# RMSNorm and matrix product on one core: TensorE's program for tiles 12 to 123 as a loop of sixteen tiles

## The chip, the cores and the metric

The kernel runs on one core of one Trainium2 chip. The metric is the device time of one execution in microseconds; the time of a kernel is the median of its runs.

## The reference

```
x: 16 x 1024 x 512 (f32)   gamma: 512   weight: 512 x 768   eps: 1e-5
rms    = sqrt(mean(x**2, axis=-1, keepdims=True) + eps)
x_norm = x / rms * gamma
out    = matmul(x_norm, weight)          # 16 x 1024 x 768, f32
```

## The kernel before

The 16,384 rows of x are 128 tiles of 128 rows. Two tiles are a pair `j`; the main loop runs over the pairs 1 to 63. Gamma is multiplied into the weights once, and the division by the rms is done on the product's rows when they leave PSUM. A tile goes through these steps:

- SyncE loads x in groups of 16 tiles (some in halves of 8) into two buffers `xt`.
- GpSimd casts x to bf16 (`cast`, into `xb`; `cast_quad`, into `xq`).
- ScalarE sums the squares of each row (`square`), two tiles at each pair, four pairs ahead, and takes the root of some tiles together (`root`); VectorE takes the reciprocal (`rstd`).
- x has to be turned so that features lie on the partitions. For 12 of every 16 tiles TensorE does it (`transpose_word`, four for each pair, strewn between the products by `feeder`) and VectorE copies the result from PSUM to `xT` (`evac`). For the last four tiles of a group of 16 (a quad, from tile 28 on) VectorE does it alone: sixteen 32x32-block transposes (`move`), three at each pair, into `xTq`.
- TensorE multiplies (`matmuls`): for each of four 128-feature slices one weight load (`hold`) and two products (`product`), 512 and 256 columns wide, into two PSUM banks that together hold a 128x768 result.
- `finish_tile` scales the result by `rstd` into `ot`: even tiles on ScalarE, odd tiles on VectorE. `store` sends eight tiles together to HBM through SyncE; the last tiles go in groups of 4, 4, 4, 2 and 2.

PSUM has three accumulators `ops` of two banks each, and two banks `tp` for transposes. `accumulator` deals the three out in turn, so a tile waits until the tile three before it has left PSUM.

Nothing is scheduled by a planner. The kernel is recorded as a list of operations with what each reads and writes (`Order.add`), in the order of the source. `Order.emit` works out which earlier operations each one has to wait for, gives each engine a semaphore that counts those of its operations that somebody waits for, and writes every engine's program straight out: 1,751 weight loads and matmuls on TensorE. Engines run their programs in order. SyncE's queue too is in order: a load that stands behind a store is issued after the store's wait has ended.

Of the kernel before, what the change touches and what calls it, by code (L numbers as in the profile page):

```python
# [11 lines left out]
F32 = mybir.dt.float32  # L12
BF16 = mybir.dt.bfloat16
# [3 lines left out]
P = 128  # L17
WIDE = 512


class Order:
# [1 line left out]

    def __init__(self, tc):  # L30
        self.tc, self.ops = tc, []

    def add(self, proc, engine, issue, reads=(), writes=()):
        self.ops.append((proc, engine, issue, list(reads), list(writes)))

    def transfer(self, engine, issue, reads=(), writes=()):
# [1 line left out]

    def emit(self):
        nc = self.tc.nc  # L40
        streams = {id(e): n for n, e in enumerate((nc.tensor, nc.vector, nc.scalar, nc.gpsimd, nc.sync))}
        writer, readers = {}, {}
        known = [dict() for _ in streams]
        clocks, needs, place, slot_of, slots = [], [], [], {}, []
        count = [0] * len(streams)
        for n, (proc, engine, _, reads, writes) in enumerate(self.ops):
            at = streams[id(engine)]
            if proc is None:
                me, turn = ("transfer", n), 1
            else:  # L50
                count[at] += 1
                me, turn = at, count[at]
            written = {writer[cell] for cell in reads + writes if cell in writer}
            read = {d for cell in writes for d in readers.get(cell, ())}
            need = []
            for d in sorted(written | read, reverse=True):
                who, when = place[d]
                if who == me and (engine is nc.tensor or d not in written):
                    continue
                if known[at].get(who, 0) < when:  # L60
                    need.append(d)
                    for k, v in clocks[d].items():
                        known[at][k] = max(known[at].get(k, 0), v)
            if proc is None:
                free = [k for k, d in enumerate(slots) if known[at].get(("transfer", d), 0)]
                if free:
                    slots[free[0]] = n
                else:
                    slots.append(n)
                slot_of[n] = ("slot", slots.index(n))  # L70
            clock = dict(known[at])
            clock[me] = turn
            place.append((me, turn))
            clocks.append(clock)
            needs.append(need)
            for cell in reads:
                readers.setdefault(cell, []).append(n)
            for cell in writes:
                writer[cell], readers[cell] = n, []
        awaited = {d for need in needs for d in need}  # L80
        seen = {who for clock in known for who in clock}
        last = [n for n, (me, _) in enumerate(place) if me not in seen and not isinstance(me, int)]
        sems, marks, done = {}, {}, {}
        for n in range(len(self.ops)):
            me = slot_of.get(n, place[n][0])
            if n in slot_of or n in awaited:
                if me not in sems:
                    sems[me] = self.tc.alloc_semaphore(f"done{len(sems)}")
                done[me] = done.get(me, 0) + (16 if n in slot_of else 1)
                marks[n] = (sems[me], done[me])  # L90
        for n, (proc, engine, issue, _, _) in enumerate(self.ops[:-1]):
            for d in needs[n]:
                engine.wait_ge(*marks[d])  # L93
            ins = issue()
            if n in marks:
                ins.then_inc(marks[n][0], 16 if n in slot_of else 1)
        return [marks[n] for n in last if n < len(self.ops) - 1], self.ops[-1][2]


@with_exitstack  # L100
def kernel(
# [8 lines left out]
    nc = tc.nc  # L110
    PE, DVE, ACT, POOL, SP = nc.tensor, nc.vector, nc.scalar, nc.gpsimd, nc.sync
    order = Order(tc)

    def run(engine, issue, reads=(), writes=()):
        order.add(1, engine, issue, reads, writes)

    x = x.flatten_outer_dims()
    out = out.flatten_outer_dims()
# [37 lines left out]
    jk = [sb(f"jk{n}", [P, D], BF16) for n in range(2)]  # L156
    xT = [sb(f"xT{n}", [P, 2, 2, P, 2], BF16) for n in range(4)]
    xq = [sb(f"xq{n}", [P, 4, D], BF16) for n in range(2)]
    xTq = [sb(f"xTq{n}", [P, 4, 2, P, 2], BF16) for n in range(2)]
    ot = [sb(f"ot{n}", [P, OG, O], F32) for n in range(3)]  # L160
    ssq = sb("ssq", [P, NT], F32)
    rms = sb("rms", [P, NT], F32)
    rstd = sb("rstd", [P, NT], F32)
# [70 lines left out]
    def evac(j, t=0, n=2):  # L234
        b = bank(j, t)
        src = tp[b].rearrange("p t h m -> p t (h m)").bitcast(BF16)
        dst = xT[j % 4].rearrange("p t h m c -> p t (h m c)")
        run(DVE, lambda: DVE.tensor_copy(out=dst[:, t:t + n, :], in_=src[:, t:t + n, :]),  # L238
            [("tp", b)], cells("xT", j % 4, t, n))
        for a in range(t, t + n):  # L240
            xT_of[2 * j + a] = (xT[j % 4][:, a], ("xT", j % 4, a))

    def transpose_tile(i):
        for h in range(2):
# [11 lines left out]
    def cast_quad(q):  # L256
        src, of = x_of(4 * q, 4)
        s = 4 * q // XG % 2
        run(POOL, lambda: POOL.tensor_copy(out=xq[s], in_=src), of, [("xq", s)])  # L259
        for t in range(4):  # L260
            xT_of[4 * q + t] = (xTq[s][:, t], ("xTq", s))
        words = xq[s].rearrange("p t d -> p (t d)").bitcast(F32).rearrange("p (a w) -> p a w", w=P)
        turned = xTq[s].rearrange("p t h m c -> p (t h m c)").bitcast(F32).rearrange("p (a m) -> p a m", m=P)
        for tokens in range(0, P, B):
            for features in range(0, P, B):
                quad_moves.append((turned[features:features + B, :, tokens:tokens + B],
                                   words[tokens:tokens + B, :, features:features + B], s))

    def move(dst, src, s):
        run(DVE, lambda: DVE.transpose(out=dst, in_=src), [("xq", s)], [("xTq", s)])  # L270

    def move_quad(n):
        for _ in range(min(n, len(quad_moves))):
# [5 lines left out]
        else:  # L279
            run(DVE, lambda: DVE.tensor_single_scalar(out=dst, in_=src, scalar=r, op=mybir.AluOpType.mult), reads, writes)  # L280

    turns = iter(range(NT + 1))

    def accumulator():
        return next(turns) % 3

    def store(i):
        first, n = o_first[i], o_size[i]
# [8 lines left out]
    def product(dst, lhsT, rhs, start, stop, reads, writes):  # L297

        run(PE, lambda: PE.add_instruction(mybir.InstMatmult(  # L299
            name=nc.get_next_instruction_name(), engine=mybir.EngineType.PE,  # L300
            ins=[PE.lower_ap(rhs), PE.lower_ap(lhsT)], outs=[PE.lower_ap(dst)],
            start_tensor_calc=start, stop_tensor_calc=stop, tile_size=(P, P), tile_position=(0, 0), ldweights=False)),
            reads, writes)

    def matmuls(i, a, ks, feed=None):
        block, cell = xT_of[i]
        for k in ks:
            lhsT = block[:, k // 2, :, k % 2]
            hold(lhsT, cell)
            for half, lo, hi in ((0, 0, WIDE), (1, WIDE, O)):  # L310
                product(ops[a][:, lo:hi], lhsT, w_bf[:, k, lo:hi], k == 0, k == K - 1,
                        [cell, ("w", k, half)], [("ops", a, half)])
            if feed:
                feed()

    def finish_tile(i, a, engine):
        s = i // OG % 3

        before = [("ot", s, i % OG - 1)] if i == o_first[i] + o_size[i] - 1 else []
        scale(engine, ot[s][:, i % OG, :], ops[a][:, :O], rstd[:, i:i + 1],  # L320
              [("ops", a, 0), ("ops", a, 1), ("rstd", i)] + before, [("ot", s, i % OG)])
        store(i)

    def feeder(pairs, gaps, alone=False):
        queue = [(j, t, h) for j in pairs for t in range(2) for h in range(2)]
# [17 lines left out]
    def load_weights(h):  # L343
# [10 lines left out]
    run(POOL, lambda: POOL.memset(ident_f, 0.0), [], ["ident"])  # L354
    run(POOL, lambda: POOL.affine_select(out=ident_f, in_=ident_f, compare_op=mybir.AluOpType.not_equal, fill=1.0, base=0,
                                         pattern=[[-1, P]], channel_multiplier=1), ["ident"], ["ident"])
    spare = accumulator()

    def warm_up(n):
        hold(warm[:, :P], "warm")  # L360
        for _ in range(n):
            product(ops[spare][:, :WIDE], warm[:, :P], warm, True, True, ["warm"], [("ops", spare, 0)])

    def weights(k, engine, lo=0, hi=O):
        halves = [half for half in range(2) if lo <= half * WIDE < hi]
# [19 lines left out]
    weights(0, DVE, 0, WIDE)  # L385
    weights(0, DVE, WIDE, O)
    weights(1, ACT)
    acc = [accumulator() for _ in range(2)]
    for i in range(2):
        matmuls(i, acc[i], [0, 1])  # L390
    weights(2, DVE)
    weights(3, ACT)
    norms(2, 2)
    cast(4, 2)
    matmuls(0, acc[0], [2, 3])
    finish_tile(0, acc[0], ACT)
    matmuls(1, acc[1], [2, 3], feeder([1], [2, 2], alone=True))
    finish_tile(1, acc[1], DVE)
    cast(6, 2)


# [2 lines left out]
    for j in range(1, NP):  # L404
# [17 lines left out]
        elif j == 3:  # L422
            feed = feeder([4, 5], both)
        elif j + 2 < NP and quad_of(j + 2) is None:
            feed = feeder([j + 2], two)
        else:
            feed = None
        for i, engine in ((2 * j, ACT), (2 * j + 1, DVE)):
            a = accumulator()
            matmuls(i, a, range(K), feed)  # L430
            finish_tile(i, a, engine)


    with tc.tile_critical():  # L434
# [45 lines left out]
```

## Time and profile before

| | |
|---|---|
| runs, device us | 208.79, 209.55, 209.25; median 209.25 |
| profiled execution, span | 207.5 us from the first to the last instruction, 1.7 us less than the median of the runs |
| busy: TensorE, VectorE, ScalarE, GpSimd | 193.3 us (93%), 149.3 (72%), 144.5 (70%), 59.8 (29%) |
| TensorE clock granted | 0.992 |
| DMA | 85.62 MB, mean 413 GB/s over the span |
| DMA queue of the loads and stores (q1) | its packets took 97.3% of 16 engines' span |
| instruction queues | q8: 7 packets, 0.11 MB; q14: 5 packets, 0.04 MB |

In the profile PE is a TensorE matmul, PEld its weight load, DVE VectorE, ACT ScalarE, POOL GpSimd and SP SyncE; L278 is line 278 of the kernel. The profile tells for each group of operations how long they were busy, how long the engine was idle ahead of them, and what ended that. It also tells for each DMA transfer when it was issued and when it had landed. A transfer of this kernel is marked as landed sixteen times, once for the share of each of the core's 16 DMA engines, and whoever waits for it waits for the last mark. Times in the trace are counted from the span's start.

### The profile page before, as it was taken

To read this page: it belongs to the slowest core of one execution; us is meant where nothing else is said; L and a number is where in the kernel's file an instruction comes from. 1 tells how busy PE (TensorE), PEld (TensorE's weight loads), DVE (VectorE), ACT (ScalarE), POOL (GpSimd) and SP (SyncE) were. 2 spreads that over 40 slices of the span, in tenths; PEclk is the share of its full clock that TensorE was granted. 3 is DMA by queue.
4 is the path that set the end of the run, shared out by engine and by line. 5 is a ranking of instruction groups with operands and counts; after the bars stand their busy time and mean duration, and the time that the engine had idled before them with its cause. 6 is when DMAs were issued, how large, how long until landed. Compare 5 with 4: busy or idle time off the path is not lost.

```text
span 207.5 us, 2761 instructions
## 1 busy us (share of the span) xinstructions
PE 193.3 (93%) x1212; PEld 72.6 (35%) x717; DVE 149.3 (72%) x255; ACT 144.5 (70%) x343; POOL 59.8 (29%) x34
## 2 busy tenths in 40 slices
PE   7779999999999999998999999999999999999940
PEld 1233434433443334342333333443334334433210
DVE  0446556999579966999379984999579984999530
ACT  4698897868777596763977877687867787683310
POOL 2156733009400291003900570006700175000000
PEclk9999999999999999999999999999999999999996
DMA  6999999999999999999999999999999999998993
GB/s 225 403 441 436 388 405 456 455 388 422 436 445 442 395 425 448 429 411 431 434 407 436 437 428 434 418 428 437 417 426 426 433 442 425 426 436 381 407 404 139
DMA packets 5632, 85.62 MB, mean 413 GB/s; under 512 B 626, under 2 KB 628, under 8 KB 1780
## 3 DMA queue, kind: packets, MB, share of 16 engines
q1 hardware_dynamic: 5616, 85.46, 97.3%
q8 instruction: 7, 0.11, 0.2%
q14 instruction: 5, 0.04, 0.0%
q10 hardware_dynamic: 4, 0.00, 0.0%
HBM read 35.13 MB, written 50.33 MB: 412 GB/s over the span
## 4 chain that ended last, share of the span: by engine, by line
PE 71%; DMA 16%; DVE 5%; issue 2%; SPq 1%; ACT 1%; POOL 1%; ACTq 0%
PE ps L299 62%; DMA xt<-in_x_dram 16%; PE ps L229 8%; DVE ot L280 2%; DVE xTq L270 2%; DVE xT L238 1%; SPq L344 1%; POOL xb L187 1%; ACT jk L195 0%; SPq L176 0%; ACT ot L278 0%; SPq L292 0%; DVE rstd L202 0%; SPq L475 0%; ACTq L93 0%
## 5 line engine op out<-in xcount | busy, mean ns | idle before, releaser
L299 PE MATMUL ps<-w_bf,xT 128*128 128x256 bf16 (+1 forms) x783 | 145.0, 325 | 3.4 <-ACT ot L278 1.3
L278 ACT ACTIVATE ot<-ps,rstd 128x768 f32<-128x768 f32 x64 | 57.4, 898 | 42.4 <-PE ps L299 40.5
L195 ACT ACTIVATE jk<-xt 128x512 bf16<-128x512 f32 x128 | 78.8, 619 | 8.3 <-DMA xt<-in_x_dram 8.2
L187 POOL CAST xb<-xt 128x2048 bf16<-128x2048 f32 (+3 forms) x21 | 46.3, 2218 | 113.2 <-DMA xt<-in_x_dram 111.4
L280 DVE TENSOR_SCALAR ot<-ps,rstd 128x768 f32<-128x768 f32 x64 | 64.8, 1013 | 9.9 <-PE ps L299 9.2
L295 PEld LDWEIGHTS <-xT 128*128 128x128 bf16 x400 | 39.3, 98 | 61.2 <-issue 53.2
L229 PE MATMUL ps<-ident_f,xb 128*128 128x128 f32 x200 | 54.4, 277 | 0.9 <-POOL xb L187 0.9
L238 DVE COPY xT<-ps 128x1024 bf16<-128x1024 bf16 (+1 forms) x53 | 34.5, 653 | 24.5 <-PE ps L229 22.8
L270 DVE STREAM_TRANSPOSE xTq<-xq 32x256 f32<-32x256 f32 x112 | 48.7, 435 | 3.4
L229 PEld LDWEIGHTS ps<-ident_f,xb 128*128 128x128 f32 x200 | 28.3, 143 | 46.5 <-issue 42.9
L299 PE MATMUL ps<-w_bf,xTq 128*128 128x256 bf16 (+1 forms) x217 | 41.8, 324 | 0.4
L195 ACT ACTIVATION_READ_ACCUMULATOR jk<-xt 128x1 f32 x128 | 24.3, 190 | 0.0
L295 PEld LDWEIGHTS <-xTq 128*128 128x128 bf16 x112 | 11.0, 98 | 14.5 <-issue 14.5
L259 POOL CAST xq<-xt 128x2048 bf16<-128x2048 f32 x7 | 13.3, 1893 | 0.0
L202 DVE RECIPROCAL rstd<-rms 128x8 f32<-128x8 f32 (+3 forms) x20 | 3.8, 192 | 7.9 <-ACT rms L200 7.7
L200 ACT ACTIVATE rms<-ssq,eps_sb 128x8 f32<-128x8 f32 (+3 forms) x20 | 6.0, 300 | 0.6
L299 PE MATMUL ps<-warm 128*128 128x512 bf16 x10 | 4.4, 582 | 1.4 <-DVE eps_sb L353 1.4
L278 ACT ACTIVATE w_bf<-w_f,g_sb 128x768 bf16<-128x768 f32 x2 | 1.9, 936 | 1.7 <-DMA w_f<-in_weight_dram 1.7
L376 DVE COPY g_sb<-ps 128x4 f32<-128x4 f32 x1 | 0.2, 163 | 3.2 <-PE ps L370 3.2
L340 ACT ACT_TABLE_LOAD x1 | 1.3, 1283 | 1.5 <-SPq L434 1.5
L280 DVE TENSOR_SCALAR w_bf<-w_f,g_sb 128x512 bf16<-128x512 f32 (+2 forms) x3 | 1.4, 481 | 1.1 <-DMA w_f<-in_weight_dram 1.1
L370 PEld LDWEIGHTS ps<-ident_f,g_row 2*128 2x128 f32 x2 | 0.3, 200 | 2.6 <-issue 2.6
(10 smaller groups left out, 2.0 us busy)
## 6 DMA issues: line engine op xcount, KB each, us to landing
out_dram<-ot SPq DMA_DIRECT2D x13, 3072.0 KB, 16.6
xt<-in_x_dram SPq DMA_DIRECT2D x9, 2048.0 KB, 21.1
xt<-in_x_dram SPq DMA_DIRECT2D x3, 4096.0 KB, 22.2
out_dram<-ot SPq DMA_DIRECT2D x4, 1536.0 KB, 11.3
out_dram<-ot SPq DMA_DIRECT2D x3, 768.0 KB, 7.0
w_f<-in_weight_dram SPq DMA_DIRECT2D x2, 768.0 KB, 5.8
xt<-in_x_dram SPq DMA_DIRECT2D x2, 512.0 KB, 5.2
xt<-in_x_dram SPq DMA_DIRECT2D x1, 1024.0 KB, 9.0
```

The source lines that it names most:

```text
L187: run(POOL, lambda: POOL.tensor_copy(out=xb[s][:, i % 8:i % 8 + n, :], in_=src), of, cells("xb", s, i % 8, n))
L195: run(ACT, lambda: ACT.activation(out=jk[j], in_=src[:, 0, :], func=AF.Square, accum_out=ssq[:, i:i + 1]), of, [("jk", j), ("ssq", i)])
L200: run(ACT, lambda: ACT.activation(out=rms[:, s], in_=ssq[:, s], func=AF.Sqrt, scale=1.0 / D, bias=eps_sb), [("ssq", t) for t in range(i, i ...
L202: run(DVE, lambda: DVE.reciprocal(out=rstd[:, s], in_=rms[:, s]), [("rms", i)], [("rstd", t) for t in range(i, i + n)])
L229: run(PE, lambda: PE.transpose(out=tp[b][:, t, h, :], in_=words[:, lo:lo + P], identity=ident_f), cells("xb", s, j % 4 * 2 + t) + ["ident" ...
L238: run(DVE, lambda: DVE.tensor_copy(out=dst[:, t:t + n, :], in_=src[:, t:t + n, :]), [("tp", b)], cells("xT", j % 4, t, n))
L259: run(POOL, lambda: POOL.tensor_copy(out=xq[s], in_=src), of, [("xq", s)])
L270: run(DVE, lambda: DVE.transpose(out=dst, in_=src), [("xq", s)], [("xTq", s)])
L278: run(ACT, lambda: ACT.mul(out=dst, in_=src, mul=r), reads, writes)
L280: run(DVE, lambda: DVE.tensor_single_scalar(out=dst, in_=src, scalar=r, op=mybir.AluOpType.mult), reads, writes)
L295: run(PE, lambda: PE.ldweights(lhsT), [cell])
L299: run(PE, lambda: PE.add_instruction(mybir.InstMatmult(name=nc.get_next_instruction_name(), engine=mybir.EngineType.PE, ins=[PE.lower_ap(r ...
```

## The change

`Order` now notes which TensorE operations belong to which turn of sixteen tiles (tiles 12 to 27 are the first, 108 to 123 the seventh) and to which half of a turn. `emit` writes TensorE's operations of the first turn once, inside a loop that runs seven times and whose head is placed at slot 0 of an instruction fetch block. TensorE's program shrinks from 1,751 weight loads and matmuls to 191 ahead of the loop, 216 in it and 48 behind it; the loop adds a counter's addition and a branch. All other engines' programs remain written out.

A loop can only wait for the same semaphore values in each turn. So:

- Operations of other engines that TensorE waits for inside the loop no longer count on their engine's common semaphore, but on one of their own for each engine and half of a turn. A product behind the last wait of a half takes the half's count off again (`taken`).
- Somebody else who waited for such an operation now waits for the next operation of that engine that is not of this kind (`shared`). For the stores this is the VectorE operation that comes after the scaling of the last tile of a group, nearly always one of the `move`s.
- Where VectorE scales the last tile of a store's group, it waited for ScalarE's scaling of the tile before. It now waits for a new small ScalarE operation behind that (`told`, one element on each partition), 20 in all.
- Each tile position of the turn has a fixed accumulator, by a list of sixteen. In it a tile takes up the accumulator of the tile three before, but for four places: the positions 6 and 8 take that of the tile two before, the positions 7 and 9 that of the tile four before. The positions 4, 6 and 8 are tiles that ScalarE scales.
- `xTq` has one buffer in place of two, and tiles 12 to 15, which TensorE transposes, use it too.

```diff
+        turns = sorted(self.body)
+        size = len(self.body[turns[0]])
 ...
+        waits = [sorted({place[d][0] for t in turns for d in needs[self.body[t][q][0]]}) for q in range(size)]
 ...
+        def shared(d):
+            if d not in events:
+                return d
+            return next(e for e in order[place[d][0]] if e > d and e not in events)
 ...
+        taken = {}
+        for (who, half), sem in own.items():
+            final = max(q for q, w in values if w == who and self.body[turns[0]][q][1] == half)
+            q = next(q for q in range(final + 1, size) if q not in flags and q not in taken and self.ops[self.body[turns[0]][q][0]][0] == "product")
+            taken[q] = (sem, -counts[who, half])
+
+        def give(n):
+            _, engine, issue, _, _ = self.ops[n]
             for d in needs[n]:
-                engine.wait_ge(*marks[d])
+                engine.wait_ge(*marks[shared(d)])
             ins = issue()
             if n in marks:
                 ins.then_inc(marks[n][0], 16 if n in slot_of else 1)
+            elif n in events:
+                ins.then_inc(own[place[n][0], events[n][1]], 1)
 ...
+        with nc.Fori(0, len(turns), engines=[mybir.EngineType.PE], head_slot={mybir.EngineType.PE: 0}):
+            for q, (n, half) in enumerate(self.body[turns[0]]):
+                for who in waits[q]:
+                    nc.tensor.wait_ge(own[who, half], values[q, who])
+                ins = self.ops[n][2]()
+                if n in marks:
+                    ins.then_inc(marks[n][0], 1)
+                elif q in taken:
+                    ins.then_inc(*taken[q])
+        for n in late:
+            give(n)
 ...
-    turns = iter(range(NT + 1))
-
-    def accumulator():
-        return next(turns) % 3
+    def accumulator(i):
+        return (2, 0, 1, 2, 0, 1, 0, 2, 0, 1, 2, 0, 1, 2, 0, 1)[(i - 12) % 16] if i >= 12 else (i + 2) % 3
 ...
-        before = [("ot", s, i % OG - 1)] if i == o_first[i] + o_size[i] - 1 else []
+        ends = i == o_first[i] + o_size[i] - 1 and i > o_first[i]
+        before = [("told", i - 1)] if ends else []
         scale(engine, ot[s][:, i % OG, :], ops[a][:, :O], rstd[:, i:i + 1],
               [("ops", a, 0), ("ops", a, 1), ("rstd", i)] + before, [("ot", s, i % OG)])
         store(i)
+        if engine is ACT and i + 1 == o_first[i] + o_size[i] - 1:
+            run(ACT, lambda: ACT.mul(out=told, in_=eps_sb, mul=1.0), ["eps"], ["told", ("told", i)])
 ...
+        order.turn, order.half = ((j - 6) // 8, (j - 6) % 8 // 4) if 6 <= j < NP - 2 else (None, 0)
```

## The prediction

> **What bounds the kernel now.** I read the page first, then who waited for whom, the stretch of one turn, and last the landing marks of the transfers. The page says that two things are nearly full at once:
>
> ```profile
> span 207.5 us, 2761 instructions
> PE 193.3 (93%) x1212; PEld 72.6 (35%) x717; DVE 149.3 (72%) x255; ACT 144.5 (70%) x343; POOL 59.8 (29%) x34
> q1 hardware_dynamic: 5616, 85.46, 97.3%
> q8 instruction: 7, 0.11, 0.2%
> q14 instruction: 5, 0.04, 0.0%
> ```
>
> TensorE is busy for 93%, the load and store queue for 97.3% of sixteen engines. The two instruction queues look like nothing: twelve packets. The waits say where TensorE loses time:
>
> ```profile
> ACT ot L278 <- PE ps L299: 40.5, 50, 1.9
> ACT jk L195 <- DMA xt<-in_x_dram: 8.2, 6, 3.6
> PE ps L299 <- ACT ot L278: 1.3, 1, 1.3
> ```
>
> That is next to nothing: one stop of 1.3 us, when ScalarE had stood 3.6 us for a late load of x. So nothing is to be won on TensorE itself. But what ends last? TensorE stops at 199.3, and the end of the trace reads:
>
> ```profile
> 199.38 1.02 DVE L280 TENSOR_SCALAR ot<-ps,rstd 128x768 f32<-128x768 f32 x1 [1.58 <-PE ps L299]
> 200.69 0.33 SPq L292 DMA_DIRECT2D out_dram<-ot  x1
> ```
>
> The last store, 768 KB, has its first landing mark at 203.9 and its last at 206.6. I took the sixteen marks of each transfer from the trace, first mark and spread from first to last, in us:
>
> ```
> transfer                  first mark   spread
> x, tiles 16 to 23              21.42     0.79
> x, tiles 24 to 31              26.65     2.51
> x, tiles 32 to 47              43.98     3.04
> x, tiles 64 to 79              92.48     4.26
> store, tiles 112 to 115       190.83     4.79
> store, tiles 126, 127         203.91     2.72
> ```
>
> The spread is 0.8 us until the first q8 packet, which starts at 27.1 us, and never less than 1.9 after it. The q8 packets are 16 KB each, start at 27.1, 50.1, 76.5, 103.5, 127.1, 151.0 and 175.9 us, and take 0.89 to 0.98 us. Following the packets of an engine back to back (the next one starts when the last ends), I find the sixteen engines' order: each q8 packet lies on another engine, and its engine falls behind by 1.3 to 1.4 us at once (at 151.0 us from 0.37 to 1.67), and by some 0.4 to 0.7 more at later loads of x. The engine that is last from 27 us on took the first q8 packet (it goes from 0.50 to 2.46) and no later one; three loads of x carry it on to 4.8. From there to the end it has no pause: the end of the kernel is this engine's backlog. The other engines do pause, about 2 us between 190 and 204. Next behind it come an engine with three of the q14 packets and one that drifts back with no fetch at all; in the last store they are 2.12 and 2.01 behind the first mark, the fourth 1.44. So TensorE has 2.7 us of room at the end: the last store could be issued that much later and the slowest engine would still be busy with earlier ones.
>
> **What it adds.** Seven additions and branches on TensorE's sequencer, and one branch to the loop's head. The nearest row is TensorE's own branch at 0.82 us, 0.17 us: 8 x 0.17 = 1.4 us in all if it lay open. [...] Branch cost: 0; without that cover 1.4 us, which the 2.7 us of room takes.
>
> The accumulators. A distance of four costs nothing. A distance of two, at 14 places, needs ScalarE to be through with a tile before TensorE has done the next. One such place is tile 96, and TensorE comes to tile 98 with the third product of the second row, at 155.92 + 0.32 = 156.24:
>
> ```profile
> 154.93 0.90 ACT L278 ACTIVATE ot<-ps,rstd 128x768 f32<-128x768 f32 x1 [0.92 <-PE ps L299]
> 155.92 0.81 PE L299 MATMUL ps<-w_bf,xT 128*128 128x512 bf16 x4
> ```
>
> ScalarE ends at 155.83: 0.41 us early. All other evacuations of these positions were released by TensorE too, with 0.92 us of idle ahead. Cost 0; if ScalarE were late by y, y - 0.41 at that place.
>
> The 20 `told` operations. Nearest rows: 0.19 us (the accumulator's reading) and 0.30 us (the root, 128x8). I take 0.25, 5 us on ScalarE, which was idle 40.5 us for TensorE and 0.58 to 0.92 ahead of the evacuations concerned. Only the last one is near the path: ScalarE ends tile 126 at 198.97, with `told` 199.2, and VectorE starts the last tile at 199.38. Cost 0, at worst 0.1.
>
> The stores wait for one more VectorE operation, a `move`, 0.435 us in its row, 16 times, and each load of x stands behind such a store in SyncE's queue, so it is issued 0.45 later. Stores land 16.6 us after issue, loads 21 us: they queue behind earlier transfers, and the slowest engine never runs dry. Cost 0; if the queue were dry, 0.45 once, since the two last stores wait as before. The single `xTq`: its first `move` stands behind the scaling of the quad's last tile on VectorE already. Cost 0.
>
> **What it removes.** [...] What that is worth depends on the engine that is last. If the fetch at 27 us goes, or lands where it does less, the next engine decides: 2.72 - 2.12 = 0.6 us. If all lag went, the last store would end 0.5 behind its first mark, as small stores do without lag (0.45 at the first load): 2.72 - 0.5 = 2.2 us. The q14 packets, which the change leaves, keep me near the lower end: 0.8 us. It must come out of the span 207.5, giving 206.7; with the 1.7 us that lie between span and median, 208.45.
>
> [...]
>
> **The rivals.** [...]
>
> (2) Slower: the fetch that stays falls on the engine that also serves the q14 packets. The six later ones were spread over six engines, so the choice moves. Price: 2.12 plus 1.3 to 2.0 is 3.4 to 4.1 us behind, against 2.72: 0.7 to 1.4 us, 209.95 to 210.65. It decides from a lag of 2.72 on.
>
> [...]
>
> (4) That the loop does not do what it says (TensorE's program still long) I rule out: 455 weight loads and matmuls are left.
>
> **How the numbers follow.** About 0.3% (0.63 us) is what a measurement of this kernel can tell from no change. Forecast, the last engine's lag falls: 0.40, value 208.45, own range 207.0 (all lag gone) to 208.65 (the next engine as it is). Rival 1: 0.33, 208.9 to 209.6. Rival 2: 0.15. Rival 3: 0.12. Faster 0.40, same 0.33, slower 0.15 + 0.12 = 0.27. The range is 207.0 to 210.6: it holds the forecast, rival 1 and nearly all of rival 2, and leaves out most of rival 3 and a gain beyond 2.2 us, some 0.15.
>
> **What would show it.** Right: q8 with two or three packets in place of seven, fewer engines more than 1 us behind, a spread in the last store of 2.1 us or less; the x load of tiles 64 to 79 landing before 96.7, and with it TensorE's stop of 1.3 us shorter (which alone doesn't move the end). Rival 1: the spread still 3.0 at tiles 32 to 47, 4.3 at tiles 64 to 79, 2.7 at the end. Rival 2: over 3.4 at the end. Rival 3: a gap of TensorE every 23.4 us and seven or more q8 packets. The prediction is wrong in its ground if the time moves by over 0.6 us while the last store's spread does not, or if TensorE waits for ScalarE once each turn.

## The result, and the profile after

The change makes the kernel slower by about 0.75 us: median 209.84 us (209.16 to 211.21) against 209.15 us (208.35 to 210.05) of the kernel before in the same measurement, a ratio of 1.0037 [1.0022, 1.0052]. The prediction said 208.45, faster; the time lies within its range, the sign is wrong. The profiled execution of the change took 210.62 us, longer than its median; a second profiled one (e1, the same kernel) took 209.44. Both are used below, and neither for a difference of the medians.

The page of the changed kernel, its busy times and DMA queues:

```profile
span 208.8 us, 2821 instructions
PE 194.5 (93%) x1236; PEld 72.7 (35%) x717; DVE 149.4 (72%) x255; ACT 146.2 (70%) x363; POOL 59.8 (29%) x34
q1 hardware_dynamic: 5616, 85.46, 97.4%
q8 instruction: 3, 0.05, 0.1%
q14 instruction: 5, 0.04, 0.0%
```

q8, whose 16 KB packets are fetches of instructions, has three packets in place of seven. ScalarE has 20 instructions more, the `told` operations. The waits of the same kernel (who waited, for whom; then us in all, times, longest):

```profile
ACT ot L348 <- PE ps L367: 41.2, 52, 1.8
ACT jk L262 <- DMA xt<-in_x_dram: 6.9, 5, 2.6
PE ps L367 <- DVE xTq L309: 1.2, 1, 1.2
PE ps L367 <- ACT ot L348: 0.4, 1, 0.4
```

TensorE's one stop for an accumulator that ScalarE had still to empty has fallen from 1.3 to 0.4 us (at 99 us in both kernels), and a new stop has come, once, for `xTq`. No wait belongs to `told` or to a branch back. Two turns of the loop, cut at the scalings of tiles 59 and 75 and of tiles 107 and 123 (length in us; the busy time of TensorE, its weight loads, VectorE, ScalarE and GpSimd; the granted TensorE clock, the busy share of the DMA engines and GB/s), first in the changed kernel and then the same tiles in the kernel before:

```profile
100.56:123.98 23.42, 23.42 (x153) 8.88 (x88) 19.07 (x33) 18.50 (x46) 9.02 (x4) 1.00 1.01 429
170.82:194.24 23.42, 23.42 (x153) 8.88 (x88) 19.07 (x33) 14.99 (x38) 3.73 (x2) 1.00 1.00 426
```

```profile
100.50:123.92 23.42, 23.26 (x150) 8.88 (x88) 19.07 (x33) 18.33 (x44) 10.00 (x5) 1.00 1.01 433
170.76:194.18 23.42, 23.26 (x150) 8.88 (x88) 19.08 (x33) 14.62 (x34) 3.27 (x2) 1.00 0.98 419
```

A turn takes 23.42 us with the loop and without (three matmul records of each turn are missing from the trace of before); in all 19 executions of the table below tile 127 is scaled 98.88 us after tile 59. TensorE's sequencer, which runs ahead of it, has these rows for the loop's branches (shortest, median and longest in ns, then the first and the last start):

```profile
L152 PEldq COMPARE_BRANCH  x8: 76/208/4585, 24.9 to 191.4; - x8
```

The six branches back take 0.21 to 0.24 us each on the sequencer and cost TensorE nothing; the shortest is the way out. The longest is the entry: the sequencer stands at it from 24.88 to 29.46 us. The end of the changed kernel:

```profile
198.94 0.19 ACT L394 ACTIVATE told<-eps_sb 128x1 f32<-128x1 f32 x1
199.44 1.02 DVE L350 TENSOR_SCALAR ot<-ps,rstd 128x768 f32<-128x768 f32 x1 [1.58 <-PE ps L367]
200.75 0.33 SPq L360 DMA_DIRECT2D out_dram<-ot  x1
```

The last store is issued at 200.75, before at 200.69. What has moved is its landing: the first mark at 203.97 (before 203.91), the last at 207.89 (before 206.63). The spread of the last store is 3.91 us in place of 2.72; 3.17 in the second profile.

### The profile page after: what moved, and what is told of

Read it like the earlier page. It is cut to its first block, busy times and chain, and to the rows that moved or that the text cites. A ratio compares the mean times of both kernels' runs of the same rounds, so it can differ in the third digit from the quotient of the medians.

```text
span 208.8 us, 2821 instructions
## 1 busy us (share of the span) xinstructions
PE 194.5 (93%) x1236; PEld 72.7 (35%) x717; DVE 149.4 (72%) x255; ACT 146.2 (70%) x363; POOL 59.8 (29%) x34
## 4 chain that ended last, share of the span: by engine, by line
PE 71%; DMA 15%; DVE 6%; issue 2%; SPq 1%; ACT 1%; POOL 1%; ACTq 0%
PE ps L367 62%; DMA xt<-in_x_dram 15%; PE ps L296 8%; DVE ot L350 2%; DVE xTq L340 2%; DVE xT L309 1%; POOL xb L254 1%; ACT jk L262 0%; SPq L416 0%; SPq L243 0%; ACT ot L348 0%; DVE xTq L309 0%; SPq L360 0%; DVE rstd L269 0%; SPq L544 0%
## 5 line engine op out<-in xcount | busy, mean ns | idle before, releaser
L367 PE MATMUL ps<-w_bf,xT 128*128 128x512 bf16 (+1 forms) x768 | 141.8, 326 | 1.4 <-DVE w_bf L350 0.9
L363 PEld LDWEIGHTS <-xT 128*128 128x128 bf16 x384 | 37.7, 98 | 58.2 <-issue 56.9
L367 PE MATMUL ps<-w_bf,xTq 128*128 128x512 bf16 (+1 forms) x256 | 49.0, 326 | 1.2 <-DVE xTq L309 1.2
L309 DVE COPY xT<-ps 128x1024 bf16<-128x1024 bf16 (+1 forms) x51 | 33.1, 652 | 23.1 <-PE ps L296 21.5
L363 PEld LDWEIGHTS <-xTq 128*128 128x128 bf16 x128 | 12.5, 98 | 17.8 <-issue 16.1
L394 ACT ACTIVATE told<-eps_sb 128x1 f32<-128x1 f32 x20 | 3.8, 192 | 0.0
L309 DVE COPY xTq<-ps 128x1024 bf16<-128x1024 bf16 x2 | 1.4, 692 | 2.4 <-PE ps L296 2.4
```

The source lines that it names most:

```text
L363: run(PE, lambda: PE.ldweights(lhsT), [cell])
L367: run(PE, lambda: PE.add_instruction(mybir.InstMatmult(name=nc.get_next_instruction_name(), engine=mybir.EngineType.PE, ins=[PE.lower_ap(r ...
```

## The experiments

Four theories stood at first. A: TensorE and with it the stores come later at tile 12, DMA engines run dry near 50 to 70 us, and the stream stays late. B: only the slowest of the sixteen DMA engines counts. C: the new accumulators, `told` and waits cost at many places. D: the loop itself costs. Ratios are to the kernel before on the same chip, 95% intervals behind them.

**e1, the change once more.** No edit.

> The changed kernel once more, beside the next three on the same chip. Theory A (TensorE stops 1.2 us at the loop's entry, because its sequencer waits for the block that holds the loop, and each store waits for one VectorE operation more; the DMA engines run out of work for 1.8 us between 50 and 70 us and never get that back): ratio to the kernel before 1.003 to 1.005, TensorE stops 1.0 to 1.5 us ahead of tile 12 again. Theory B (only the lag of the slowest DMA engine decides, by where the fetches fall): the ratio moves between chips, 1.000 to 1.006. Theory C (the new waits and accumulators cost a little everywhere): 1.0037.

1.0032 [1.0013, 1.0051]: the loss is there again. **e2**, the loop's head at slot 14 in place of slot 0:

```diff
-        with nc.Fori(..., head_slot={mybir.EngineType.PE: 0}):
+        with nc.Fori(..., head_slot={mybir.EngineType.PE: 14}):
```

> [...] Theory A: no stop of TensorE ahead of tile 12, two q8 packets in place of three, the first landing mark of the x load of tiles 48 to 63 near 68.8 us instead of 70.1; ratio to before 0.997 to 1.000. Theory B: the stop goes, the time stays, 1.002 to 1.005, unless the slowest engine's lag moves with it. Theory C: 1.0037.

1.0040 [1.0025, 1.0055], three q8 packets as in the change: the place of the head is not the cause.

**e3, the change with its loop written out**: all waits, accumulators and buffers of the change, but seven turns of code.

```diff
-        with nc.Fori(0, len(turns), ...):
-            for q, (n, half) in enumerate(self.body[turns[0]]):
+        for k, t in enumerate(turns):
+            for q, (n, half) in enumerate(self.body[t]):
-                    nc.tensor.wait_ge(own[who, half], values[q, who])
+                    nc.tensor.wait_ge(own[who, half], values[q, who] + k * counts[who, half])
 ...
```

> All of the change (semaphores of their own, accumulators in an order of sixteen, one xTq, told, the stores' later wait) without the loop: TensorE's seven turns are written out, with counts that go on rising. Theory A: no stop at tile 12, seven q8 packets, the stream of transfers 0.4 to 0.6 us late at the x load of tiles 48 to 63 from the stores' wait alone, the lag as before: ratio 1.001 to 1.003. Theory B: 1.000. Theory C: 1.0037.

1.0015 [1.0003, 1.0027]. More than half of the loss goes with the loop. The new stop at tile 12 has two parts, which the timelines show; the changed kernel first:

```profile
28.04 0.69 DVE L309 COPY xTq<-ps 128x1024 bf16<-128x1024 bf16 x1 [1.42 <-PE ps L296]
29.52 0.10 PEld L363 LDWEIGHTS <-xTq 128*128 128x128 bf16 x1 [1.69 <-DVE xTq L309]
```

Then e3, written out:

```profile
28.53 0.69 DVE L307 COPY xTq<-ps 128x1024 bf16<-128x1024 bf16 x1 [1.42 <-PE ps L294]
29.27 0.10 PEld L361 LDWEIGHTS <-xTq 128*128 128x128 bf16 x1 [0.95 <-DVE xTq L307]
```

Tile 12 waits for the copy of tiles 14 and 15, since the four tiles now share the one cell `xTq`. Written out, TensorE goes on 0.05 us after that copy has ended; in the loop 0.79 us after it (29.52 less 28.73), though the view names the copy for both. The sequencer's row above gives the rest of the wait: its branch into the loop ends at 29.46, 0.06 ahead of the weight load. By the scalings of tiles 11 and 13, which lie 3.04 us apart before, the stop is 1.37 us in the changed kernel, 1.01 in e1, 1.38 in e2 and 0.63 in e3: the shared cell is 0.63, the entry into the loop 0.4 to 0.75 (in e7 and e6 below it is 0.3 and 0; in e6 the branch ends ahead of the copy). Nothing of it repeats in later turns.

**e4, the kernel before with a stop put in**: a weight load and six products of zeros ahead of tile 12. **e5, the loop from tile 28**, six turns, tiles 12 to 15 back in `xT`. The edits of e4 and of e5 (of e5 the main line):

```diff
+            if i == 12:
+                hold(warm[:, :P], "warm")
+                for _ in range(6):
+                    product(ops[a][:, :WIDE], warm[:, :P], warm, True, True, ["warm"], [("ops", a, 0)])
```

```diff
 ...
-        order.turn, order.half = ((j - 6) // 8, (j - 6) % 8 // 4) if 6 <= j < NP - 2 else (None, 0)
+        order.turn, order.half = ((j - 14) // 8, (j - 6) % 8 // 4) if 14 <= j < NP - 2 else (None, 0)
```

> The kernel before, with one weight load and six products of 128x512 more (zeros, 1.3 us) on TensorE ahead of tile 12; nothing else. Theory A: the stores of tiles 8 to 23 leave 1.3 us later, the DMA engines run dry and the end moves by 1.0 to 1.3 us: ratio 1.005 to 1.006. Theory B, and the prediction's 2.7 us of room at the end: 1.000. Theory C says nothing on it.

> The loop begins one turn later: tiles 12 to 27 are written out, the loop covers tiles 28 to 123 in six turns, and tiles 12 to 15 go through xT again. Theory A, as the first four runs leave it (up to the store of tiles 16 to 23 the DMA engines wait for the stores, so a late TensorE moves all that follows; after it they never run dry. Late by 0.73 us for tile 12 waiting on the second pair in xTq, 0.4 to 0.75 for the loop's entry, 0.38 for the store waiting on a move): that store is issued near 48.7 us as in the kernel before, the stop at the entry comes at tile 28, where it is hidden; ratio 0.998 to 1.001. Theory D (the loop itself costs, by its fetches and by what its turns add): 1.002 to 1.004.

e4: 1.0017 [1.0004, 1.0030]; the load of x for tiles 48 to 63 begins to land at 69.24 in place of 68.21, so a shift of 1.0 us goes with 0.17%, 0.36 us (0.1 to 0.6 by the interval). e5: 1.0029 [1.0012, 1.0047], though that load lands at 68.28 and no stop is left. Theory A has a part of the loss at most. **e6** split the stores of the second and third group of eight in halves to have them leave sooner, **e8** did the same in the kernel before, **e7** let the stores wait for a small VectorE operation straight behind the scaling:

```diff
-    o_first, o_size = stretches(OG, {0: [1, 1, 2, 4], ...
+    o_first, o_size = stretches(OG, {0: [1, 1, 2, 4], 1: [4, 4], 2: [4, 4], ...
```

```diff
+    said = sb("said", [P, 1], F32)
 ...
+        if ends:
+            run(DVE, lambda: DVE.memset(said, 0.0), [], ["said"])
         store(i)
```

> The changed kernel with the stores of tiles 8 to 15 and 16 to 23 in halves of four tiles, nothing else: the DMA engines get the first half some 6 us earlier. The stops of TensorE stay. Theory A: the x load of tiles 48 to 63 has its first landing mark near 68.3 us instead of 69.5 to 70; ratio 0.998 to 1.001. Theory D: 1.003.

> The kernel before with the same split stores as in the run named split. In it the DMA engines ran dry for 0.14 us at that place, and not at all where TensorE stopped 1.3 us near 98 us. Theory A: little to gain, ratio 0.998 to 1.000. Theory D: 1.000. Should it gain as much as the split does in the changed kernel, the split acts otherwise than by closing the gap.

> The changed kernel with a one-element memset on VectorE behind each scaling that ends a store's group, so that the store waits for this and not for the next move. Theory A: the store of tiles 16 to 23 is issued 0.35 us earlier than in the changed kernel with the same stops, the time falls by 0.1 to 0.3: ratio 1.001 to 1.003. Theory D: 1.003 to 1.004, as 16 more operations on VectorE bring nothing.

e6: 1.0040 [1.0028, 1.0053], no gain; e8: 1.0025 [1.0006, 1.0043], so the split costs by itself. Its cost has a reason in the traces: the load of tiles 32 to 47 now stands behind one more store in SyncE's queue and is issued at 31.45 in e6 (25.96 in the change) and at 30.70 in e8 (26.38 in the kernel before). In e6 the load of tiles 48 to 63 does begin to land early, at 68.39, but that of tiles 64 to 79 begins 1.29 us later than in the kernel before, in e8 1.40. So e6 says nothing against theory A. e7: 1.0023 [1.0008, 1.0038], some 0.1% below the change and e1, with intervals that overlap.

**e9, the loop from tile 28, written out** (the edits of e3 and e5 together). **e12, the loop from tile 28 with e7's edit.** All three kernels from tile 28 (e5, e9, e12) share the accumulators and `told`; e5 and e9 differ by the loop alone.

> The change with the loop from tile 28 and with the loop written out: the accumulators' order, the 20 told operations, the stores' wait for one more VectorE operation and the single xTq of the quads remain; the stop at tile 12, the loop and its fetches are gone. Measured against the loop from tile 28 (209.54, ratio 1.0029). Theory A (late stores let the DMA engines run dry; the loop itself is free): the stores' 0.37 us remain, worth about 0.1 us, so 209.25, and the loop from tile 28 has no reason to lie higher. Theory D (the loop itself costs, through its two close fetches and the one at its exit): 209.15 to 209.25, 0.3 us below the loop from tile 28, with seven q8 packets in place of four. Theory C (accumulators at distance two, told): as the loop from tile 28, 209.5.

> The loop from tile 28, and the stores wait for a small VectorE operation straight behind the scaling in place of the next move. No stop at tile 12, no late store: what is left of the change is the loop with its fetches, the accumulators' order and told. Theory A: as before, 209.15. Theory D: as the loop from tile 28, 209.4 to 209.55. Theory C: the same 209.4 to 209.55; the written out loop from tile 28 of this same set tells C from D.

e9: 1.0006 [0.9989, 1.0022]. e12: 1.0023 [1.0007, 1.0039]. Theory C falls: accumulators, `told`, the single `xTq` and the stores' wait from tile 28 on cost nothing that the measurement tells from zero. The loop, with the stop at tile 12 and the late stores taken away, still costs (e5 1.0029, e12 1.0023).

**e10, one cell for tiles 12 to 15, in the kernel before. e11 and e16, late stores in the kernel before**, which wait for the third VectorE operation behind the scaling that ends their group:

```diff
+        to = ["first"] * 2 if j in (6, 7) else cells("xT", j % 4, 0, 2)
...
-            xT_of[2 * j + a] = (xT[j % 4][:, a], ("xT", j % 4, a))
+            xT_of[2 * j + a] = (xT[j % 4][:, a], to[a])
```

```diff
+        def behind(n, d):
+            if self.ops[n][1] is not nc.sync or place[d][0] != streams[id(nc.vector)] or n < late_from:
+                return d
+            return vector[min(vector.index(d) + 3, len(vector) - 1)]
 ...
```

> The kernel before, with one thing of the change: the turned tiles 12 to 15 stand as one cell, so tile 12 waits for the copy of tiles 14 and 15 too. TensorE should stop 0.7 us at tile 12 and everything behind it come 0.7 later: the store of tiles 16 to 23 issued near 49.4 (before 48.7), the x load of tiles 48 to 63 landing near 68.9 (before 68.2). Theory A: 0.3 us of time for each us of this shift (as the products put in ahead of tile 12 cost 0.3 for 1.0), so 209.35. Theories B and D: no change, 209.15.

> The kernel before, whose stores from tiles 8 to 15 on (all but the last two) wait for the third VectorE operation behind the scaling that ends the group, where the change makes them wait for the first. The first costs 0.37 us in the changed kernel, so the third about 1.2 us at each store. Theory A: the x load of tiles 48 to 63 lands 1.2 later, near 69.4, and the time goes up by some 0.4, to 209.5; the change's own 0.37 is then worth 0.1. Theories B and D: no change, 209.15.

> The stores' wait once more, on the kernel before: the stores of tiles 8 to 111 wait for the third VectorE operation behind the scaling that ends the group; the last five stores are left as they were (in the run before this, the store of tiles 120 to 123 waited for an operation at the very end, and the last three stores left together, which is what its 2.7 us were). If the slowest engine absorbs late stores (theory B and theory D): 209.15, as the single cell brought nothing (1.0002) for 0.7 us. Theory A: 209.5, and the change's own 0.37 us are worth 0.1.

e10: 1.0002 [0.9989, 1.0015], with its stop of 0.63 us in the trace; but in the profiled execution tile 11 came 0.50 us earlier, and the load of tiles 48 to 63 began only 0.22 later than in the kernel before. e11: 1.0128 [1.0103, 1.0152] says nothing on the question: the store of tiles 120 to 123 waited for an operation at the very end and began to land at 204.67 in place of 200.15. e16, which leaves the last five stores alone: 1.0014 [1.0002, 1.0027]. The issues of the store of tiles 16 to 23 and of the load behind it, in the kernel before, in the changed one, and in e16:

```profile
48.70 0.33 SPq L292 DMA_DIRECT2D out_dram<-ot  x1
49.07 0.46 SPq L176 DMA_DIRECT2D xt<-in_x_dram  x1
```

```profile
50.11 0.33 SPq L360 DMA_DIRECT2D out_dram<-ot  x1
50.49 0.43 SPq L243 DMA_DIRECT2D xt<-in_x_dram  x1
```

```profile
49.38 0.33 SPq L302 DMA_DIRECT2D out_dram<-ot  x1
49.75 0.66 SPq L186 DMA_DIRECT2D xt<-in_x_dram  x1
```

Counted from the scaling of tile 11 (29.07, 28.65 and 28.33) the store is issued after 19.63, 21.46 and 21.05 us: 1.83 later in the change, 1.42 later in e16. By the clock of the traces, in which tile 11 comes earlier in both, the load is issued 1.42 and 0.68 later, and its first mark comes 1.83 and 0.72 later (68.21, 70.04, 68.93). So at about 50 us a later issue is a later landing. Behind it nothing is added, though e16's stores wait at every group: at the store of tiles 104 to 111 the first mark is 1.84 and 0.65 later. And the slowest engine makes it good: the last mark of the store of tiles 104 to 111 comes at 191.97 in the kernel before, at 191.49 in e16, 191.81 in e3 and 191.78 in e4 (193.23 in the change, 192.05 in e1).

What of the loop costs, then? D1: the two fetches close together at its entry. D2: the fetch at its exit, near 194 us. D3: the branches back. To tell these apart, loops of other lengths and places: **e13**, two turns from tile 28; **e14**, the last two turns; **e15**, six loops of one turn, each with its own code; **e17**, four turns from tile 28; **e18**, the last four.

```diff
-        order.turn, order.half = ((j - 14) // 8, ...) if 14 <= j < NP - 2 else (None, 0)
+        order.turn, order.half = ((j - 14) // 8, ...) if 14 <= j < 30 else (None, 0)        # e13; e17: < 46
+        order.turn, order.half = ((j - 46) // 8, ...) if 46 <= j < NP - 2 else (None, 0)    # e14; e18: 30
```

```diff
-        with nc.Fori(0, len(turns), ...):
-            for q, (n, half) in enumerate(self.body[turns[0]]):
+        for t in turns:
+            with nc.Fori(0, 1, ...):
+                for q, (n, half) in enumerate(self.body[t]):
```

> The loop from tile 28 (209.54 to 209.57, ratios 1.0029 and 1.0023), with two turns only (tiles 28 to 59); the rest written out. It enters as before at 49 us with its two close fetches (49 and 56), leaves at about 96 us instead of 194, and from there fetches a block every 25 us again. Theory D1 (the two close fetches at the entry put two engines behind early, and their lag grows with each later load of x): as the loop of six turns, 209.5. Theory D2 (what costs is at the end: the fetch at the exit near 194 us falls where no time is left to make it good): 209.15 to 209.25. Theory D3 (each branch back costs): a fifth of it, 209.2.

> The loop for tiles 92 to 123 alone, two turns; the program ahead is written out, with a q8 packet every 25 us as in the kernel before. The entry with its close fetches is at about 147 us, the exit at 194 us as in the loops before. Theory D1: the lag has only 45 us and three loads of x to grow, so 209.2. Theory D2: as the loops that end there, 209.5. Theory D3: 209.2.

> The loop from tile 28 as six loops of one turn each, every turn with its own code: the same order of work and the same waits, but six entries with their close fetches in place of one, so some twelve q8 packets in place of four. Theory D1: each entry puts two more engines behind; 209.5 at least, and 210 or more if the later ones add up. Theory D2: 209.5 too, as the last exit is the same. Theory D3: no branch goes back, 209.15. If the fetches are harmless in themselves and it is their absence that costs (the other engines are no longer held up, and only the last one counts), 209.15.

> The loop from tile 28 with four turns (tiles 28 to 91), exit at about 145 us. With two turns there the time was 1.0009 of before, with six 1.0029 and 1.0023. Theory P (the cost grows with the stretch in which the single fetches are missing: from the load of tiles 64 to 79 to the store of tiles 104 to 111 the eighth of the sixteen landing marks comes 1.2 us sooner in the loops that run to the end, but the last mark takes 96.0 us in place of 95.5): about 1.0015, with the eighth mark 0.6 us sooner. Theory D2 (the exit fetch near the end costs): 1.0005. Theory D1 (the close fetches at the entry): 1.0025, as with six turns.

> The loop for tiles 60 to 123, four turns, entry at about 98 us and exit at 194 us. Theory P: about 1.0015, as the four early turns. Theory D2: 1.0025, as the loops that end there (against it, the two late turns, 1.0003). Theory D1: 1.0005, as the lag of the engines hit at the entry has less time to grow.

All kernels but e11 in one table; each row but the ratio is one profiled execution. "8th" and "last" are the time that the eighth and the last of the sixteen landing marks take from the load of tiles 64 to 79 to the store of tiles 104 to 111; "behind" counts the engines more than 1 us behind the first there; "end" is the last mark of the last store.

```
kernel                         ratio    q8   8th    last   behind   end
before                                   7   95.88  95.23   10    206.63
e9   written out from 28       1.0006    7   95.82  95.23   10    206.64
e3   written out from 12       1.0015    7   95.83  95.42   11    206.58
e4   before, stop              1.0017    7   95.77  95.65   11    206.68
e8   before, split             1.0025    7   95.69  95.25   10    206.73
e10  before, one cell          1.0002    7   95.83  96.11   10    206.44
e16  before, late stores       1.0014    7   95.38  95.19   10    206.42
e13  two turns early           1.0009    7   95.98  95.07   10    206.41
e14  two turns late            1.0003    7   95.73  95.85    9    206.25
e15  six loops of one turn     1.0029    9   95.61  95.76   11    207.07
e17  four turns early          1.0024    5   95.07  96.26    8    207.12
e18  four turns late           1.0018    5   94.71  96.07    7    206.41
e5   six turns                 1.0029    4   94.65  95.69    6    206.60
e12  six turns, e7's edit      1.0023    4   94.66  96.00    6    206.97
the change                     1.0037    3   94.65  96.43    5    207.89
e1   the change again          1.0032    3   94.69  95.67    5    206.71
e2   slot 14                   1.0040    3   94.65  95.97    6    207.70
e6   the change, split         1.0040    3   94.68  95.39    5    207.49
e7   stores behind a mark      1.0023    3   94.64  96.23    5    207.42
```

The ratios of e17 and e18 are 1.0024 [1.0006, 1.0043] and 1.0018 [1.0005, 1.0031], of e13 and e14 1.0009 [0.9997, 1.0021] and 1.0003 [0.9989, 1.0016], of e15 1.0029 [1.0009, 1.0049]. The queues of e18 and of e15:

```profile
q1 hardware_dynamic: 5616, 85.46, 97.3%
q8 instruction: 5, 0.08, 0.2%
```

```profile
q1 hardware_dynamic: 5616, 85.46, 97.1%
q8 instruction: 9, 0.15, 0.3%
```

D2 falls as the common cause: e17 leaves its loop near 147 us and costs as much as e12, e14 leaves it at 193.9 and costs nothing. D1 falls: e18 enters at 102.4 without a second fetch close by, and still loses; e13 enters with two (50.1 and 56.3) and loses little. D3 falls as a cost on TensorE by the 23.42 us of each turn.

What is left (theory P of the last two expectations) is the length of the stretch without single fetches: none or two turns 1.0002 to 1.0017 (e15 and the split of e8 aside), four to seven 1.0018 to 1.0040. In that stretch the eighth mark gets on up to 1.2 us faster, by the more the more fetches are gone, and the last mark does not: in the nine executions with four turns or more it takes 95.97 us in the mean, in the ten others 95.48 (standard deviations 0.33 and 0.35), and the end comes at 207.15 against 206.59. Two executions of one and the same kernel, the change and e1, lie 0.76 us apart in this column and 1.18 at the end, and the intervals of neighbouring ratios overlap, so the step from two turns to four is shown by the set of them and by no pair. That the missing fetches cause it is what is left, and was not shown by itself.

e15 does not fit P, having nine fetches, but its trace has a reason of its own: its last fetch, at 194.3, follows straight on the packets of an engine that is already 3.6 us behind the first mark, and the last mark falls from 4.00 to 5.25 us behind between that store and the next.

## Why the prediction was wrong

**What bounds the kernel** held. TensorE ended as early as before (and in e15 1.1 us earlier, in a slower kernel), and each profiled execution ended 2.7 us behind the last store's last landing mark.

**What it removes** is the step that failed, in its size and its sign. The count of packets was right (its signs had two or three, three came in place of seven), though an estimate of the author's: how many instructions a packet holds no run shows; in the kernel before the seven packets start 252 weight loads and matmuls apart in the mean. Right too was what fewer packets do: the engines more than 1 us behind fall from ten to five, the eighth mark gains 1.2 us. The error was to let this reach the end. The step took 0.8 us "if the fetch at 27 us goes, or lands where it does less". It did neither: in the changed kernel and in e1 the packet at 27 us is still there, and its engine is still one of the two last at the end. Rival 1, at 0.33, was that the fetch at 27 us stays, on the same engine, with no change as the result. It missed that entering the loop brings a second packet 6 us after the first (33.0 us in place of 50.1; the loop has been running since 29.5), and that this engine joins the first one: in the last store they are 3.9 and 3.7 us behind the first mark (3.2 and 3.2 in e1), and the engine that drifts with no fetch 3.4 (3.0). The six fetches from 50.1 us on, in place of which two came (33.0 and 194.1), had been on engines that did not decide. The lag at the end grew from 2.72 to 3.91 us (3.17 in e1) where the step had it fall. That the range still held the time is owed to rivals 1 and 2, which it took in, and not to the mechanism of the forecast.

The nine executions with the longer loops also have a slower last engine, by 0.49 us over that stretch (95.97 less 95.48). Its lag grows at the loads of x: on the engine with the first fetch, between the loads of tiles 64 to 79 and the store of tiles 104 to 111, by 1.64 us in the changed kernel, 1.05 in e1 and 1.01 in e5, against 0.56 in the kernel before and 0.47 in e9. The two sets overlap: e10, without a loop, takes 96.11 us, and the engine with its first fetch falls back by 1.25, from 3.02 us behind. Why an engine that is late loses more when fewer of the others are late, no run here shows. That the others run further ahead of it, and it alone then has the old transfer while they are at the next, is a guess. It could be tested by holding up the middle engines in another way than by fetches, which was not tried.

**What it adds.** "Branch cost: 0" is right for the branches back (0.21 to 0.24 us each on the sequencer, more than the 0.17 that it reckoned with, and all hidden) and wrong for the entry: the sequencer stood at it for 4.6 us, when TensorE had 3.2 us of queued work (from 24.88 to 28.06, where its last product ahead of tile 12 starts). The cover that the step counted on was the author's estimate, which no run before the change showed; at the entry it was these 3.2 us. Of the 1.4 us that were left the wait for the shared cell covered about half; 0.74 lay open (0.4 in e1), once. For the single `xTq` the step looked at the quads and overlooked tiles 12 to 15, where the one cell makes tile 12 wait 0.63 us; in time it was nothing (e10). The accumulators at distance two and `told` (0.19 us each, 3.8 in all, estimate 5) cost nothing, as said (e9). For the stores it said 0 as "the slowest engine never runs dry": TensorE's stop and the stores' wait together bring the first mark of the load of tiles 48 to 63 1.83 us later, and the last engine makes nearly all of it good. e16, with a first mark 0.72 later, and e4, with 1.03, measure 1.0014 and 1.0017; the change lies 0.0008 to 0.0014 above the loops without the shift (e5, e12), and e3 0.0009 above e9. So it is some 0.2 to 0.3 us of the 0.75, not 0, and the loop has the rest. This split is not firm: at e4's price the shift of 1.83 would alone be worth 0.65 us, an estimate, and with the 0.5 to 0.6 us of e5 and e12 that is more than the whole loss.

**Rival 2** comes nearest in time (from 209.95), but a fetch on an engine that also has q14 packets is not the change's mechanism: the engine of the packet at 33.0 has none. That a fetch on an engine that is already late costs, e15 seems to show, with an end of 207.07 after the earliest last mark of the store of tiles 104 to 111 of all (191.43). **Rival 3**, a fetch at every branch back, did not happen: three packets in all, none of which starts between 33.1 and 194.1 us, and no gap at a turn of 23.42 us.

## What to carry to other kernels

Where the end is set by the last of several parallel engines, a saving counts only if it falls on that one: follow that engine's own history (here the fetch at 27 us and the loads of x) and ask whether the change touches it. Taking disturbances off the others can look right in every count and gain nothing. When a loop replaces written out code, look at what the loop forces on data and waits at its first turn, as well as at its branches.

## What the runs showed of the hardware

- An instruction fetch of 16 KB cost TensorE nothing (a turn is 23.42 us with it and without) but put one of the sixteen DMA engines behind: in the kernel before the last landing mark lies 0.79 us behind the first at the load of tiles 16 to 23, ahead of the fetch at 27.1 us, and 2.51 us at the next load, and the engines more than 1 us behind are six ahead of the fetch at 127.1 us and seven after it. The lag stayed until the stream of transfers ran out: from 27.1 us on the last mark lies 1.93 to 4.85 us behind the first, at the last store 2.72.
- In the kernels with fewer such fetches the middle of the sixteen engines was up to 1.2 us faster over 96 us and the last of them 0.5 us slower in the mean; the cause stays open.
- The entry into the loop held TensorE's sequencer for 3.3 to 4.6 us at tile 12 (the change, e1, e2, e6, e7) and TensorE itself for 0 to 0.75 us. The view of waits ascribed all of it to the VectorE copy, which in the change had ended at 28.73, 0.79 us before TensorE went on at 29.52; the sequencer's row, with the branch's end at 29.46, tells the rest.
- The entry at tile 28 held the sequencer for 2.0 to 2.9 us. In e5 it cost TensorE nothing (23.42 us from tile 27 to tile 43, as in the kernel before); in e12, e17, e15 and e13 the same stretch took 0.13, 0.24, 0.34 and 0.36 us more, and the first weight load of tile 28 came 0.05 to 0.06 behind the branch's end. The later entries of e14, e15 and e18 took the sequencer 0.3 us.
